# A hybrid short-convolution and state-space trunk on one core: the short mixer's output pairs for the first half of the sequence move ahead of the second half's input pairs, and the scan's first half is stored in seven forms

## The chip, the cores and the metric

One core of a Trainium2 chip. The metric is the device time of one execution in microseconds (us). TensorE is PE in the profile, its weight loads are PEld, VectorE is DVE, ScalarE is ACT, GpSimd is POOL. SP is the queue that issues nearly all transfers (DMAs) here.

## The reference, cut to what matters

Input x is 2048 positions by 1024 channels, f32. One layer and a closing norm:

```python
h = rmsnorm(x, norm_mix_w)
u_b, u_c, u_h, z, xbc, dt_raw = split(h @ w_in)          # w_in: 1024 x 5648
y_a = u_b * causal_conv3(u_c * u_h)                        # the short mixer, 1024 wide
xs, bm, cm = split(silu(causal_conv4(xbc) + conv_b))       # the scan's inputs
dt = softplus(dt_raw + dt_bias)
y = ssd_scan(xs, dt, -exp(a_log), bm, cm) + d_skip * xs    # 16 heads of 64, 2 groups, chunked
y_b = rmsnorm_per_group(y * silu(z), ssd_norm_w)           # 1024 wide, 2 groups of 512
x = x + concat(y_a, y_b) @ w_out                           # w_out: 2048 x 1024
x = x + relu(rmsnorm(x, norm_mlp_w) @ w_up) ** 2 @ w_down  # 4096 wide
out = rmsnorm(x, final_norm_w)
```

## The kernel before

**Layout.** Channels lie on the 128 partitions, positions along the free dimension. The sequence is cut into two halves of 1024 positions (h = 0, 1), each of two blocks of 512 (b = 0, 1 and b = 2, 3). All products are f32: each operand is split into a high and a low part (`whi`, `wlo` for weights, `uh`, `ul` for data), and three matmuls of 128x128 by 128x512 make one product (lines 293, 294, 295 in `chain`, lines 133 to 135 in `mm3`).

**Seven products for eight.** A "pair" is two output tiles of 128 channels over both blocks of a half: a 2x2 block product. `Seven.chain` does it with seven block products instead of eight, in the order b11, t1, t2, b21, t3, b22, t4. One product is 4 places of three matmuls, so a pair is 84 matmuls. For it the data must be there in seven forms, sums and differences of the four blocks (`uh0..uh3`, `ul0..ul3`: places 0 to 2 hold two forms each, place 3 the seventh), and the weights in four forms (`combine` makes the sums `s12`, `s34`). Results leave PSUM in `evict`, on DVE or ACT, product by product. The PSUM tiles px and py are each used by several products in turn, so a later product waits until the earlier one's result has been read.

**Stages.** (1) `first_half`: 20 pairs of w_in for h = 0. Pairs named ch and b make the short mixer and store its output in seven forms (`y7_d`); x pairs make the scan's inputs (`xs_d`); z pairs store silu(z) (`sz_d`). (2) `second_half`: the 22 pairs of `LATER` for h = 1, then 8 pairs o0 to o7 (`OUTS`) that multiply the short mixer's output by the first 1024 rows of w_out: o0 to o3 for h = 0, o4 to o7 for h = 1. Their results are added to x and stored in `x1_d`. (3) `Output`: 32 "units", one for each output tile of 128 channels and block of 512, which multiply the scan's output by the other rows of w_out: 8 places of three matmuls, 24 matmuls a unit, no sevens (PSUM tile pm). Units 0 to 15 are for b = 0, 1, units 16 to 31 for b = 2, 3. They add to `x1_d`; those of b = 0, 1 also add up the squares for the next norm. (4) The MLP, its two halves, and the closing norm.

**Turns.** Between groups of pairs the data operand changes. `renew` loads the seven forms of the next operand into the places as the last pair before frees them (L354: `ul<-y_d`), ACT makes the high part (L361) and DVE the low part (L362); places 2 and 3 are done in the next pair (`renew_rest`). There are two such turns in `second_half` (z4 to o0, o3 to o4), one change of the input half (`refresh`, at the end of the first half), and one into the units (`enter`).

**The scan** (`Scan`) runs beside the products on all engines. A chunk is 128 positions of one group of 8 heads; there are 32. `front` and `back` are generators that are advanced a step at a time (8 steps a chunk) from `after`, which `chain` calls behind each product: normally 8 steps a pair, fewer at a turn. On PE a chunk is the transposes ptx and ptb, the state product st, then yo, yd and, for its norm, pss. 27 chunks (`SPLIT`) run in `second_half` with single buffers (pool sp1). The last 5 run in the units 0 to 12 with a second pool (sp2, double buffers). Each chunk stores its gated and normalised output in `yn_d` (L1673).

**What sets the order.** The program is written in the order that the generators give, and a scheduling layer then places each instruction in its engine's queue. Each engine takes its own queue in order. SP's queue of DMAs is one such queue: a DMA that waits holds back those behind it.

Of the kernel before, what the change touches and what calls it, by code (L numbers as in the profile page):

```python
# [16 lines left out]
P = 128  # L17
T = 2048
D = 1024
TB = 512  # L20
# [19 lines left out]
def trunk(ctx: ExitStack, tc: tile.TileContext, x, x_tok, w_in, w_dt, w_out, w_up, w_down, cvec, hrow, out):  # L40
# [21 lines left out]
    xs_d, sz_d, yn_d = wide("xs", 12), wide("sz", 8), wide("yn", 8)  # L62
# [150 lines left out]
    class Seven:  # L213
# [158 lines left out]
        def prepare(self, h, src, base, accs=None, held=None):  # L372
# [32 lines left out]
            for k in range(4):  # L405
                ts = [held("nb") if held and i == 2 else self.raw("nb") for i in range(4)]
# [15 lines left out]
                if held:  # L422
                    self.held.append(ts[2])
                    nc.sync.dma_start(self.stored[h][k][:, 2:4], ts[1])
                    self.settle([self.places[k]], 0, [ts[0]])
# [29 lines left out]
    class Proj(Seven):  # L455
# [5 lines left out]
        LATER = "z6 x0 z0 ch0 ch4 b0 x8 ch1 ch5 b1 x2 ch2 ch6 b2 x10 z2 x4 x6 ch3 ch7 b3 z4".split()  # L461
        OUTS = "o0 o1 o2 o3 o4 o5 o6 o7".split()
# [30 lines left out]
        def tmp(self, name):  # L493
            return self.up.tile([P, TB], F32, tag="utmp", name=name, bufs=4 - 2 * self.h)
# [244 lines left out]
        def dt_weights(self):  # L739
# [3 lines left out]
            if self.h == 0:  # L743
                wdt = self.sumtile("wdt").bitcast(F32R)[:, 0 : KD * 32]
            else:
                wdt = self.up.tile([P, KD * 32], F32R, name="wdt")
# [106 lines left out]
        def pair(self, h, what, ws, ahead, after):  # L853
# [13 lines left out]
            elif kind == "o":  # L867
                return self.out_pair(n, ws, ahead, after)
# [70 lines left out]
        def residual(self, n, b):  # L939

            t = self.e("x0") if b == 0 else self.up.tile([P, TH], F32, tag="cc", name="x1", bufs=2)
            self.res[n, b] = t
            at = 2 * (n % 4)
            nc.sync.dma_start(t.rearrange("p (a t) -> p a t", a=2), x[n // 4 * NBB + b, :, at : at + 2])

        def out_pair(self, n, ws, ahead, after):
            b0, b1 = (self.res.pop((n, b)) for b in range(NBB))
# [3 lines left out]
            def evict(name, gi, pm):  # L951
# [10 lines left out]
                if fin:  # L962
                    nc.sync.dma_start(x1_d[n // 4 * NBB + b][:, 2 * (n % 4) + i], t)

            return self.chain([self.places], ws, ahead, evict, after)

        def renew(self, h, name):
# [3 lines left out]
            if name in ("t1", "b21", "b22", "t4"):  # L971
                i = ("t1", "b21", "b22", "t4").index(name)
                for k in range(4):
                    self.land(i, k, y7_d[h][k][:, 2 * i : 2 * i + (1 if i == 3 else 2)])
# [14 lines left out]
        def weights(self, h, what):  # L989

            if h == 0:
                if what != self.LATER[0]:
                    sums_d[what] = dram.tile([P, 2, 1024], F32, name=f"sums_{what}_d")
                raws = self.load_cols(w_in, self.cols(what))()
                yield
                yield from self.combine(*raws, sums_d.get(what))
# [12 lines left out]
            else:  # L1009
                f0, f1 = self.cols(what)  # L1010
            raw = lambda n, w=1024: wp.tile([P, 1024], F32, tag="wraw", name=n, bufs=3)[:, 0:w]
            r0 = load_w(w[f0])
            if what not in sums_d:
                r1 = load_w(w[f1])
                yield
                yield from self.combine(r0, r1)
                return
            s12, s34 = raw("s12"), raw("s34")
            nc.sync.dma_start(s12, sums_d[what][:, 0])
            nc.sync.dma_start(s34, sums_d[what][:, 1])  # L1020
# [3 lines left out]
            nc.sync.dma_start(a22.rearrange("p (k c) -> p k c", c=P), w[f1][:, KD // 2 :])  # L1024
# [3 lines left out]

        def first_half(self, ws):
            self.last_sums()  # L1030
            late = self.prepare(1, x, C_NMIX)
            for m, what in enumerate(self.PAIRS):
                last = m + 1 == len(self.PAIRS)
                if last:
                    for _ in late:
                        pass
                    ahead = None
                    self.new = [{} for _ in range(4)]
                else:
                    ahead = self.weights(0, self.PAIRS[m + 1])  # L1040
# [7 lines left out]
                ws = self.pair(0, what, ws, ahead, after) or ws  # L1048
# [3 lines left out]
        def second_half(self, ws, side):  # L1052

            self.dt_weights()
            dts = itertools.chain(*(self.dt_part(NBB + bb) for bb in range(NBB)))
            self.res = {}
            order = self.LATER + self.OUTS
            nl = len(self.LATER)
            turn = lambda m: m - nl in (-1, 3)
            for m, what in enumerate(order):  # L1060
                last = m + 1 == len(order)
                ahead = self.plain(w_out[1], (0, 1)) if last else self.weights(1, order[m + 1])

                def after(name):
                    if m or name == "t4":
                        next(dts, None)
                    at = m - nl
                    rest = at in (0, 4)
                    if name in LIGHT if turn(m) else name in LATE if rest else True:
                        for _ in range(1 + (name == "t3")):  # L1070
                            next(side, None)
                    if turn(m):
                        self.renew((at + 1) // 4, name)
                    elif rest:
                        self.renew_rest(name)
                    if m + 1 >= nl and not last and name in ("t1", "t3"):
                        self.residual(m + 1 - nl, ("t3", "t1").index(name))
# [4 lines left out]
                if turn(m):  # L1082
# [419 lines left out]
    SPLIT = 27  # L1502
    LIGHT, LATE = ("b11", "t3"), ("t3", "b22", "t4")

    class Scan:
# [45 lines left out]
        def load_rows(self, n):  # L1551
# [6 lines left out]
            if self.bufs == 1:  # L1558
                eb = self.tile([4, L], "eb", 1)
            else:  # L1560

                eb = uh.tile([P, 1, TB], F32R, tag="uh3", name="eb", bufs=4).bitcast(F32)
                eb = eb[:, 0].rearrange("p (j l) -> p j l", j=4)
            self.got[n]["eb"] = eb
# [54 lines left out]
        def back(self, n):  # L1619
# [22 lines left out]
            y = t["y"]  # L1642
# [360 lines left out]
```

## Time and profile before

| what | value |
|---|---|
| median of 3 runs | 2591.67 us (2590.14 to 2596.16) |
| the profiled execution's own time | 2592.11 us |
| its span | 2590.1 us |
| granted TensorE clock | 1.0 |
| PE busy, weight loads busy | 99%, 81% of the span |
| DVE, ACT busy | 75%, 54% |
| read and written in HBM | 364 MB, 187 MB |

PE's busy time is modelled: a matmul's record lasts longer than the time until the next one starts, so a stage is better judged by when its matmuls start and by what is left idle.

### The profile page before, as it was taken

To read this page: it belongs to the slowest core of one execution; us is meant where nothing else is said; L and a number is where in the kernel's file an instruction comes from. 1 tells how busy PE (TensorE), PEld (TensorE's weight loads), DVE (VectorE), ACT (ScalarE), POOL (GpSimd) and SP (SyncE) were. 2 spreads that over 40 slices of the span, in tenths; PEclk is the share of its full clock that TensorE was granted. 3 is DMA by queue.
4 is the path that set the end of the run, shared out by engine and by line. 5 is a ranking of instruction groups with operands and counts; after the bars stand their busy time and mean duration, and the time that the engine had idled before them with its cause. 6 is when DMAs were issued, how large, how long until landed. Compare 5 with 4: busy or idle time off the path is not lost.

```text
span 2590.1 us, 33610 instructions
## 1 busy us (share of the span) xinstructions
PE 2567.3 (99%) x11962; PEld 2109.2 (81%) x11962; DVE 1947.4 (75%) x2677; ACT 1405.0 (54%) x2171; POOL 66.5 (3%) x97
## 2 busy tenths in 40 slices
PE   9999999999999999999999999999999999999999
PEld 7888888778888887778888888888888888888887
DVE  7888776777888879778767765655558877877875
ACT  7554345776577765547336555655556444444443
POOL 0011000000000000000000000000000000000001
PEclk9999999999999999999999999999999999999999
DMA  5557535555656669989765774744448766676872
GB/s 215 204 202 278 204 139 185 186 179 189 194 172 198 193 220 313 328 272 285 239 211 183 261 255 147 259 143 159 154 147 284 260 203 207 225 236 218 281 252 78
DMA packets 295623, 553.87 MB, mean 214 GB/s; under 512 B 26272, under 2 KB 142496, under 8 KB 295456
## 3 DMA queue, kind: packets, MB, share of 16 engines
q1 hardware_dynamic: 295024, 551.34, 62.7%
q8 instruction: 94, 1.54, 0.2%
q14 instruction: 73, 0.60, 0.1%
q10 hardware_dynamic: 432, 0.39, 0.0%
HBM read 364.46 MB, written 187.17 MB: 213 GB/s over the span
## 4 chain that ended last, share of the span: by engine, by line
PE 85%; DMA 6%; DVE 5%; ACT 2%; issue 1%; SPq 0%; DVEq 0%; ACTq 0%
PE px L293 14%; PE px L295 14%; PE px L294 14%; PE py L293 7%; PE py L295 7%; PE py L294 7%; PE pw L293 3%; PE pw L295 3%; PE pw L294 3%; PE pm L133 3%; PE pm L134 3%; PE pm L135 3%; PE pm L510 1%; PE yd L1635 1%; PE yo L1632 1%
## 5 line engine op out<-in xcount | busy, mean ns | idle before, releaser
L293 PE MATMUL px<-uh,whi 128*128 128x512 f32 x1800 | 705.0, 392 | 3.4 <-DVE x L961 1.5
L294 PE MATMUL px<-ul,whi 128*128 128x512 f32 x1800 | 701.7, 390 | 0.2 <-DVE ul L362 0.2
L295 PE MATMUL px<-uh,wlo 128*128 128x512 f32 x1800 | 700.6, 390 | 0.6 <-DVE wlo L110 0.6
L293 PEld LDWEIGHTS px<-uh,whi 128*128 128x128 f32 x1800 | 337.9, 188 | 78.3 <-DVE acc L1314 2.8
L295 PEld LDWEIGHTS px<-uh,wlo 128*128 128x128 f32 x1800 | 337.9, 188 | 71.9 <-DVE wlo L110 1.7
L294 PEld LDWEIGHTS px<-ul,whi 128*128 128x128 f32 x1800 | 338.0, 188 | 70.0 <-DVE ul L362 1.8
L109 ACT CAST whi<-s 128x1024 fp32r<-128x1024 f32 (+1 forms) x222 | 232.2, 1046 | 276.2 <-PE py L294 147.5
L110 DVE TENSOR_TENSOR wlo<-wraw,whi 128x1024 fp32r<-128x1024 f32 (+1 forms) x220 | 219.5, 998 | 184.5 <-ACT whi L109 182.7
L293 PE MATMUL py<-uh,whi 128*128 128x512 f32 x900 | 354.7, 394 | 1.4 <-ACT s L1111 0.8
L295 PE MATMUL py<-uh,wlo 128*128 128x512 f32 x900 | 351.6, 391 | 0.0
L294 PE MATMUL py<-ul,whi 128*128 128x512 f32 x900 | 351.0, 390 | 0.0
L110 DVE TENSOR_TENSOR wlo<-s,whi 128x1024 fp32r<-128x1024 f32 (+1 forms) x222 | 269.8, 1215 | 70.7 <-ACT whi L109 69.4
L109 ACT CAST whi<-wraw 128x1024 fp32r<-128x1024 f32 (+1 forms) x220 | 191.9, 872 | 226.1 <-PE px L294 163.4
L293 PEld LDWEIGHTS py<-uh,whi 128*128 128x128 f32 x900 | 169.0, 188 | 39.5 <-issue 3.3
L295 PEld LDWEIGHTS py<-uh,wlo 128*128 128x128 f32 x900 | 169.0, 188 | 35.6 <-issue 0.3
L294 PEld LDWEIGHTS py<-ul,whi 128*128 128x128 f32 x900 | 169.0, 188 | 34.1 <-issue 0.2
L349 DVE TENSOR_TENSOR ul<-rh,uh 128x1024 fp32r<-128x1024 f32 (+1 forms) x128 | 138.7, 1086 | 49.6 <-ACT uh L348 49.2
L293 PE MATMUL pw<-uh,whi 128*128 128x512 f32 x450 | 175.4, 390 | 0.0
L295 PE MATMUL pw<-uh,wlo 128*128 128x512 f32 x450 | 175.3, 390 | 0.0
L294 PE MATMUL pw<-ul,whi 128*128 128x512 f32 x450 | 175.3, 389 | 0.0
L348 ACT CAST uh<-rh 128x1024 fp32r<-128x1024 f32 (+1 forms) x128 | 119.9, 944 | 92.7 <-PE py L295 57.3
L301 ACT COPY pw<-px 128x512 f32<-128x512 f32 x118 | 67.6, 573 | 114.3 <-PE px L295 113.1
(261 smaller groups left out, 3672.4 us busy)
## 6 DMA issues: line engine op xcount, KB each, us to landing
hid_d<-e SPq DMA_DIRECT2D x96, 512.0 KB, 3.6
rh<-hid_d SPq DMA_DIRECT2D x96, 512.0 KB, 4.6
wraw<-w_in SPq DMA_DIRECT2D x67, 512.0 KB, 4.5
wraw<-w_up SPq DMA_DIRECT2D x62, 512.0 KB, 4.4
wraw<-w_down SPq DMA_DIRECT2D x88, 256.0 KB, 4.2
dec<-rd_d SPq DMA_DIRECT2D x32, 512.0 KB, 5.1
wraw<-w_out SPq DMA_DIRECT2D x28, 512.0 KB, 5.8
x<-x SPq DMA_DIRECT2D x24, 512.0 KB, 6.8
```

Of the source, the lines that this page charges most:

```text
L109: nc.scalar.copy(hi, raw)
L110: eng.tensor_tensor(out=lo, in0=raw, in1=hi.bitcast(F32), op=ALU.subtract)
L133: nc.tensor.matmul(out, whi, hi, start=(k == 0), stop=False)
L134: nc.tensor.matmul(out, whi, lo, start=False, stop=False)
L135: nc.tensor.matmul(out, wlo, hi, start=False, stop=(k == nk - 1))
L293: nc.tensor.matmul(p, hi, h[0], start=bool(first and k == 0), stop=False, **kw)
L294: nc.tensor.matmul(p, hi, h[1], start=False, stop=False, **kw)
L295: nc.tensor.matmul(p, lo, h[0], start=False, stop=(k == len(g) - 1), **kw)
L301: self.copied = nc.scalar.copy(pm[gi]["w"], pm[gi]["x"]).ins
L348: nc.scalar.copy(p[i][0], t)
L349: nc.vector.tensor_tensor(out=p[i][1], in0=t, in1=p[i][0].bitcast(F32), op=ALU.subtract)
L510: last[engine] = make(*args, **kw).ins
```

## The change

1. Order of `second_half`: o0 to o3 (`FORMER`) come first, then `LATER` in another order, then p0 to p3 and o4 to o7. The first half now ends with a turn to the short mixer's output (`y7_d[0]`), and `second_half` has three turns: o3 to x0 (the second input half, `hm_d[1]`, whose seven forms the first half stored as before), b3 to p0 (the scan's first half, `yb7`), p3 to o4 (`y7_d[1]`).
2. p0 to p3 are new pairs: the scan's output for h = 0 times its rows of w_out, by seven products. They replace units 0 to 15. They take `x1_d` as what is added to, and also do the squares for the next norm (`square`).
3. The scan writes its first half (b = 0, 1) in the seven forms (`yb_d`) instead of `yn_d`: chunks of b = 0 store two forms, chunks of b = 1 load those again (into the tile xd), make four differences on DVE and store them.
4. `gate_weights`, in the first half, multiplies the scan's rows of w_out by ssd_norm_w, makes the weight sums and stores them (`wy_d`). Before, the gain was applied to the data (`cut`).
5. One scan pool: all 32 chunks run in `second_half` with single buffers. What is left of the scan before the last pair, o7, is written at once ahead of it. z pairs advance the scan by 10 steps instead of 8.
6. The units left are 16, for b = 2, 3, two output tiles at a time in the order (2, d), (2, d+1), (3, d), (3, d+1). The MLP's preparation runs beside them as before, and holds back place 0 instead of place 2 until unit 13.

The instructions counted in the two programs: 384 matmuls of the units go (128 in each of three lines) and 336 of pairs come; DMAs go from 1505 to 1590, DVE instructions from 2679 to 2763, ACT instructions from 2167 to 2180.

```diff
     def __init__(self): ...
-        LATER = "z6 x0 z0 ch0 ch4 b0 x8 ch1 ch5 b1 x2 ch2 ch6 b2 x10 z2 x4 x6 ch3 ch7 b3 z4".split()
-        OUTS = "o0 o1 o2 o3 o4 o5 o6 o7".split()
+        LATER = "x0 z0 x8 z2 x2 ch0 ch4 x10 b0 z4 ch1 ch5 x4 b1 z6 x6 ch2 ch6 b2 ch3 ch7 b3".split()
+        FORMER = "o0 o1 o2 o3".split()
+        OUTS = "p0 p1 p2 p3 o4 o5 o6 o7".split()
...
         def first_half(self, ws):
-            late = self.prepare(1, x, C_NMIX)
+            late = itertools.chain(self.prepare(1, x, C_NMIX), self.gate_weights())
...
-                        self.refresh(name)
+                        self.renew(y7_d[0], name)
...
         def second_half(self, ws, side):
-            order = self.LATER + self.OUTS
-            turn = lambda m: m - nl in (-1, 3)
+            order = self.FORMER + self.LATER + self.OUTS
+            nf, nl = len(self.FORMER), len(self.FORMER) + len(self.LATER)
+            turns = {nf - 1: hm_d[1], nl - 1: yb7, nl + 3: y7_d[1]}
...
-                        for _ in range(1 + (name == "t3")):
+                        for _ in range(1 + (name == "t3") + (what[0] == "z" and name in ("t1", "b21"))):
                             next(side, None)
...
+                    if not last and order[m + 1][0] in "op":
+                        at = {"t4": (1, 0)} if what[0] == "b" else {"t1": (1,), "t3": (0,)}
+                        for b in at.get(name, ()):
+                            self.residual(order[m + 1], b)
...
+                if last:
+                    for _ in side:
+                        pass
...
         # in Scan.back, at the end
-            nc.sync.dma_start(yn_d[h][:, 4 * g : 4 * g + 4, ts], y)
+            if h:
+                nc.sync.dma_start(yn_d[:, 4 * g : 4 * g + 4, ts], y)
+                yield
+                return
...
+            if b == 0:
+                for i in range(2):
+                    put(3 * i, 1, y[:, 2 * i : 2 * i + 2])
+            else:
+                yp, s = t["xd"], self.tmp().rearrange("p (j l) -> p j l", j=4)
+                sub(s[:, lo], y[:, lo], yp[:, lo])
+                sub(y[:, lo], y[:, hi], y[:, lo])
+                sub(s[:, hi], y[:, hi], s[:, lo])
+                sub(t4, yp[:, hi], s[:, hi])
+                put(1, 2, s)
+                put(4, 2, y)
+                put(6, 1, t4)
...
         # in Output
-        UNITS = [(b, d) for d in range(KD) for b in ((0, 1) if d < 7 else (1, 0))] + [(b, d) for d in range(KD) for b in (2, 3)]
+        UNITS = [(b, d + i) for d in range(0, KD, 2) for b in (2, 3) for i in range(2)]
...
-            side = scan.run(0, SPLIT)
+            side = scan.run(0, len(CHUNKS))
             ws = proj.second_half(ws, side)
...
-            scan.open(c2, "sp2", 2)
-            side = scan.run(SPLIT, len(CHUNKS))
-            for n in range(13):
-                proj_out.unit(n, hook)
```

**On DVE, at the turn into the first output pairs behind the input pairs.** Before, this is z4 to o0; `x<-py` and `x<-px` (L961) empty o0's PSUM tiles, `ul` of L362 are the low parts of the new operand, the 128x512 ones those of place 3.

```order
L362 TENSOR_TENSOR ul_8599<-ul_8599,uh_8598 128x1024
L961 TENSOR_TENSOR x_8548<-py,x_8548 128x512
L1652 TENSOR_TENSOR state_3787<-state_3787,dd 128x512
L1654 TENSOR_TENSOR stmp<-yo,eb 128x512
L961 TENSOR_TENSOR x_8548<-px,x_8548 128x512
L362 TENSOR_TENSOR ul_8668<-ul_8668,uh_8667 128x1024
L1653 TENSOR_TENSOR state_3787<-state_3787,st 128x512
L362 TENSOR_TENSOR ul_8671<-ul_8671,uh_8670 128x1024
L961 TENSOR_TENSOR x_8642<-pw,x_8642 128x512
L362 TENSOR_TENSOR ul_8674<-ul_8674,uh_8673 128x1024
```

After, it is b3 to p0; L985 empties p0's PSUM tiles and L366 makes the low parts.

```order
L366 TENSOR_TENSOR ul_9729<-ul_9729,uh_9728 128x1024
L366 TENSOR_TENSOR ul_9732<-ul_9732,uh_9731 128x1024
L366 TENSOR_TENSOR ul_9735<-ul_9735,uh_9734 128x1024
L366 TENSOR_TENSOR ul_9762<-ul_9762,uh_9761 128x512
L366 TENSOR_TENSOR ul_9765<-ul_9765,uh_9764 128x512
L366 TENSOR_TENSOR ul_9768<-ul_9768,uh_9767 128x512
L1725 TENSOR_TENSOR stmp<-stmp 128x256
L366 TENSOR_TENSOR ul_9771<-ul_9771,uh_9770 128x512
L1727 TENSOR_TENSOR ssq<-stmp 128x128
L985 TENSOR_TENSOR x_9777<-py,x_9777 128x512
L985 TENSOR_TENSOR x_9777<-px,x_9777 128x512
```

The first two evictions stood ahead of the low parts of places 2 and 3; now they stand behind all of them.

**On PE, where the scan ends.** Before, a late chunk's products (st, yo, yd) stand among the matmuls of a unit (pm), and the norm's pss of the chunk ahead of it follows.

```order
L135 MATMUL pm<-uh_10186,wlo 128x512
L133 MATMUL st<-xde,btok 128x512
L134 MATMUL st<-xde,btok 128x512
L135 MATMUL st<-xde,btok 128x512
L1632 MATMUL yo<-bc,state_3788 128x128 x4
L1635 MATMUL yd<-dec,stmp 64x128 x8
L1667 MATMUL pss<-ssq,ones_r 128x128
L133 MATMUL pm<-uh_10177,whi 128x512
```

After, the last two chunks stand in the last pair, o7 (its first product writes this px): chunk 30's products and already the transposes of chunk 31.

```order
L1730 MATMUL pss<-ssq,ones_r 128x128
L297 MATMUL px<-uh_10447,whi 128x512
L298 MATMUL px<-ul_10448,whi 128x512
L299 MATMUL px<-uh_10447,wlo 128x512
L297 MATMUL px<-uh_10450,whi 128x512
L137 MATMUL st<-xde,btok 128x512
L1651 MATMUL ptx<-ident,xd 128x128 x4
L298 MATMUL px<-ul_10451,whi 128x512
L1691 MATMUL yo<-bc,state_3889 128x128 x4
L138 MATMUL st<-xde,btok 128x512
L139 MATMUL st<-xde,btok 128x512
L1694 MATMUL yd<-dec,stmp 64x128 x8
```

Chunk 31's own yd stands 42 large matmuls further on, still in o7; before, a late chunk's yd stood 48 behind the one ahead of it.

**On SP, behind the last chunk.** Before, the scan's last store (L1673) is followed by the units' own transfers, and only units from the 17th on read what it stores. After, L1737 is that store and L1810 loads it for the units of b = 3.

```order
L1673 DMA yn_d_102<-y 128x4x128
L1828 DMA x_d_77<-xt 128x512
L1755 DMA ry<-yn_d_102 128x2x512 x2
L1801 DMA xt<-x_d_77 128x512
L1828 DMA x_d_78<-xt 128x512
```

```order
L1737 DMA yn_d<-y 128x4x128
L105 DMA wraw<-w_out 128x1024
L1840 DMA xt<-x_d_79 128x512
L1810 DMA ul_11441<-yn_d 128x2x512
L1810 DMA ul_11444<-yn_d 128x2x512
L1810 DMA ul_11447<-yn_d 128x2x512
L1810 DMA ul_11450<-yn_d 128x2x512
```

The loads stand two rows behind the store, and the third unit, the first of b = 3, reads them.

More of the change, by code (lines that the diff above doesn't have):

```diff
@@ L866, in pair @@
                 nc.gpsimd.tensor_copy(b[:, 0:2], self.halo_s[:, n, :])
[L867 to L868 removed]
+            elif kind in "op":
+                return self.out_pair(what, ws, ahead, after)
             else:
@@ L1045, in after @@
                     if last:
-                        self.refresh(name)
-                ws = self.pair(0, what, ws, ahead, after) or ws
+                        self.renew(y7_d[0], name)
+                ws = self.pair(0, what, ws, ahead, after)
             self.places = self.new
```

287 lines of the change are left out of this document (135 added, 152 removed).

## The prediction

> **What bounds the kernel now.** First the page: span, busy shares, chain.
>
> ```profile
> span 2590.1 us, 33610 instructions
> PE 2567.3 (99%) x11962; PEld 2109.2 (81%) x11962; DVE 1947.4 (75%) x2677; ACT 1405.0 (54%) x2171; POOL 66.5 (3%) x97
> PE 85%; DMA 6%; DVE 5%; ACT 2%; issue 1%; SPq 0%; DVEq 0%; ACTq 0%
> ```
>
> PE is the bound at full clock; DVE is the next engine. Since PE's busy time is modelled, I looked up when pairs start. Columns: start, duration, engine, operation.
>
> ```profile
> 308.16 0.39 PE L293 MATMUL pw<-uh,whi 128*128 128x512 f32 x1
> 327.20 0.39 PE L293 MATMUL pw<-uh,whi 128*128 128x512 f32 x1
> ...
> 702.56 0.39 PE L293 MATMUL pw<-uh,whi 128*128 128x512 f32 x1
> 725.41 0.39 PE L293 MATMUL pw<-uh,whi 128*128 128x512 f32 x1
> ```
>
> The first two are one pair apart without scan work: 327.20 - 308.16 = 19.04 us for 84 matmuls, 0.2267 us each. The last two are one pair with one chunk of the scan apart, 22.85 us, so a chunk takes 3.81 us of PE. A matmul removed is worth 0.2267 us, not its recorded 0.39.
>
> Then the stages: first half, its last turn, two early stretches of the second half, its steady part, the output pairs with their turns, the units with the scan's last 5 chunks, the units without. Columns: window, its length, busy time of PE, PEld, DVE, ACT, POOL, PE clock, DMA share, GB/s.
>
> ```profile
> 79.00:441.00 362.00, 361.63 (x1598) 298.97 (x1597) 285.34 (x359) 167.14 (x210) 32.56 (x38) 1.00 0.55 196
> 441.00:490.00 49.00, 47.88 (x229) 36.88 (x228) 34.72 (x51) 38.67 (x70) 2.09 (x2) 1.00 0.77 253
> 490.00:545.00 55.00, 53.05 (x276) 41.50 (x275) 43.60 (x90) 42.52 (x72) 1.01 (x4) 1.00 0.49 155
> 545.00:952.00 407.00, 405.23 (x2124) 334.05 (x2123) 333.28 (x470) 272.41 (x516) 17.25 (x34) 1.00 0.59 185
> 952.00:1144.00 192.00, 186.77 (x917) 150.70 (x916) 155.05 (x216) 109.95 (x187) 0.00 (x0) 1.00 0.90 313
> 1144.00:1242.00 98.00, 95.97 (x519) 79.62 (x518) 80.71 (x129) 60.60 (x130) 0.00 (x0) 1.00 0.87 274
> 1242.00:1336.00 94.00, 94.00 (x417) 77.82 (x416) 67.42 (x89) 25.78 (x33) 0.00 (x0) 1.00 0.72 242
> ```
>
> Idle time of PE is length less busy: 0.37, 1.12, 1.95, 1.77, 5.23, 2.03 and 0.00 us, 12.1 us from 441 on. That is all the waiting that the changed part can lose; it may also grow. Inside the output pairs:
>
> ```profile
> 960.00:1003.00 43.00, 40.83 (x194) 32.11 (x193) 41.27 (x55) 33.51 (x49) 0.00 (x0) 1.00 0.91 324
> 1060.00:1084.00 24.00, 23.27 (x112) 17.84 (x111) 20.90 (x27) 13.95 (x16) 0.00 (x0) 1.00 0.81 321
> 1084.00:1144.00 60.00, 57.67 (x290) 46.81 (x290) 41.22 (x63) 26.81 (x56) 0.00 (x0) 1.00 0.87 285
> ```
>
> The turn z4 to o0 costs 2.17 us, with DVE busy 41.27 of 43 us; o3 to o4 costs 0.73; entering the units 2.33.
>
> **The change, part by part.** *Matmuls.* 384 go, 336 come: 48 x 0.2267 = -10.9 us. The scan's matmuls are unchanged. The squares' matmuls change line, not number.
>
> *DVE in the first half and the scan.* The rows that price DVE, and those of ACT that a chunk waits for (line, engine, tiles, count, then total us and mean ns):
>
> ```profile
> L232 DVE TENSOR_TENSOR nb<-nb 128x512 f32<-128x512 f32 x16 | 10.5, 685 | 0.0
> L1662 DVE TENSOR_TENSOR stmp<-stmp 128x256 f32<-128x256 f32 x32 | 13.4, 419 | 5.3 <-ACT stmp L1661 5.1
> L362 DVE TENSOR_TENSOR ul<-ul,uh 128x1024 fp32r<-128x1024 f32 x24 | 28.7, 1217 | 0.9 <-ACT uh L361 0.9
> L362 DVE TENSOR_TENSOR ul<-ul,uh 128x512 fp32r<-128x512 f32 x8 | 5.1, 682 | 0.0
> L961 DVE TENSOR_TENSOR x<-px,x 128x512 f32<-128x512 f32 x24 | 16.5, 685 | 4.7 <-PE px L295 4.6
> L1616 DVE TENSOR_TENSOR dec<-dec,smask 128x1024 f32<-128x1024 f32 x32 | 39.0, 1220 | 9.9 <-ACT dec L123 9.8
> L1672 DVE TENSOR_TENSOR y<-y,ssq 128x512 f32<-128x512 f32 x32 | 21.9, 684 | 10.0 <-ACT ssq L1670 9.9
> L1610 ACT ACTIVATE dec<-dec,dd 128x128 f32<-128x128 f32 x256 | 85.4, 392 | 25.8 <-DMA dec<-rd_d 25.0 <-DMA dd<-dt_d 0.7
> L123 ACT ACTIVATE dec<-dec 128x1024 f32<-128x1024 f32 x32 | 33.9, 1059 | 0.6
> L123 ACT ACTIVATE ssq<-pss,hb 128x128 f32<-128x128 f32 x32 | 11.6, 363 | 6.9 <-PE pss L1667 6.8
> L1670 ACT ACTIVATE ssq<-ssq 128x128 f32<-128x128 f32 x32 | 9.8, 307 | 0.6
> L1781 ACT ACTIVATE uh<-ul,cv 128x512 fp32r<-128x512 f32 x16 | 10.4, 712 | 7.4 <-DMA ul<-yn_d 7.4
> ```
>
> `gate_weights` adds 32 DVE instructions of 128x512, the size of the `nb` row: 32 x 0.685 = 22 us. DVE there goes from 285 to 307 of 362 us, 85%; PE still waited only 1.77 us in the steady stretch where DVE was 82% busy (333.28 of 407). I take nothing, and keep 1 us. The differences of `yb_d`: 8 chunks x 4 instructions of 128x256 at 0.419 us = 13.4 us in the steady part, which has some 70 us of DVE left over: nothing. If that cover went, up to 13 us would show. The load of `xd` back from `yb_d` is needed only at the chunk's end, behind the scan's other work: nothing.
>
> *z pairs at 10 steps* move scan work earlier and change no sum.
>
> *Turn z6 to o0* (the end of the first half). The first evictions (two of 0.685) stand behind the low parts again, and the scan has hardly begun, so I take about what the turn of the input half cost (1.12) to what z4 to o0 cost (2.17): 2 us at most, 1.2 taken.
>
> *New turn o3 to x0.* Before there was none inside these pairs. Nearest row: the input half's turn, 1.12. Bounds 0.7 and 2.2; 1.1 taken.
>
> *Turn b3 to p0.* On DVE, behind b3's last product, now come its eviction, a weight's low part and t24 (3 x 0.685), six splits of 1.217, four of 0.682, two small ones (0.42, 0.2) and only then p0's first eviction (0.685): 2.1 + 7.3 + 2.7 + 0.6 + 0.7 = 13.4 us. PE has 48 matmuls (10.9) and the scan's transposes, 12.0 us in all, before it needs that PSUM tile. On SP the residual stands behind the last loads of the operand, which stand behind the store of t24, which waits on DVE. Transfers in the crowded stretch, from the chain (start, duration, transfer):
>
> ```profile
> 1047.27 9.02 DMA x<-x
> ...
> 1065.41 7.65 DMA ul<-y_d
> ...
> 1103.70 4.95 DMA yn_d<-y
> ...
> 1134.28 5.81 DMA ul<-yn_d
> ```
>
> 2.3 us of DVE until t24, then 9.02 for a residual, then the eviction: 12.0, about the same cover, if it lands like that row. So 1.5 us by DVE alone, more with queueing: bounds 1 and 6, 4 taken, since the similar old turn had a shorter DVE row and paid 2.17.
>
> *Turn p3 to o4.* As o3 to o4 (0.73) plus up to 4 squares of 0.685 on DVE: 0.7 to 3.4, 1.2 taken. Two steady waits of about 2 us (490:545, 545:952) stay: 2 + 2.
>
> *The scan's end.* The pairs offer 241 steps, the scan needs 4 + 32 x 8 = 260; 19 steps, 2.4 chunks, are written at once ahead of o7. From yd of chunk 30 to yd of chunk 31: the decay's load, 4.95 (the nearest transfer of that size), 8 activations (0.392 alone, some 0.31 apart when back to back: 2.5 to 3.1), exponential 1.06, mask 1.22 = 10.0 us; PE has 42 matmuls, 9.5. Behind the last pss: 0.36 + 0.31 + 0.68, store 4.95, load 5.81, scaling 0.71 = 12.8 us against 42 matmuls, 9.5. So 0.5 + 3.3, and about 1 for queueing: 5 us, where the entry into the units and their part with the scan cost 2.33 + 2.03 = 4.4. Bounds: 2 (the load lands early) and 10 (each of the three transfers takes some 2 to 3 us longer, as 9.02 against 5.81).
>
> Waits after: 1.2 + 4 + 1.1 + 4 + 1.2 + 5 = 16.5 us, against 12.1: +4.4. Sum: -10.9 + 4.4 = -6.5. Against the profiled execution's own 2592.11 (2 us outside its span) that gives 2585.6; the median of the runs is 0.4 lower, so 2585.2 to 2585.6, **2585.5 us**. About 0.2%, 5.2 us, can be told from no change: faster is below 2586.5, slower above 2596.9.
>
> Transfers as a bound: the output stretch already moves 313 GB/s at 0.90. By the program's tile sizes about 62.5 MB now move there instead of about 60 (313 x 192), over some 200 us: no new bound, but no room.
>
> PE's weight loads weigh on whether removing matmuls saves time at all:
>
> ```profile
> L293 PEld LDWEIGHTS px<-uh,whi 128*128 128x128 f32 x1800 | 337.9, 188 | 78.3 <-DVE acc L1314 2.8
> ```
>
> A load of 188 ns in each 226.7 ns is 83%, so the page's 81% is what an unbroken stream shows here. The Trainium skill, "Perfetto Trace Analysis", section "Identifying the Most-Contended Engine", holds the share of LDWEIGHTS, not of matmuls, to be the measure of closeness to the limit, by which 81% would leave room. The trace doesn't bear that out. By the Trainium skill, "TensorE: Matmul & The Clock Gate", section "Back-to-back issue gap", sustained matmuls of N = 512 come about 131 ns apart: 48 of them would be an estimated 6.3 us rather than 10.9. No stretch of this trace has them that close; the starts above are 226.7 apart.
>
> **The rivals.**
> *R1, turns and end eat the gain.* Four turns at 2.2 to 6 and the end at its worst: 2.2 + 2.2 + 6 + 2.2 + 8 + the steady 4 = 24.6, less 12.1, = +12.5 at the extreme; a middle course, waits of 21 to 22, gives 2592.1 - 10.9 + 9.5 = 2590.7. For it: DVE at 41.27 of 43 us. Against: each turn so far cost at most 2.3.
> *R2, slower: the drained scan.* From yd of chunk 29 to the first unit of b = 3 runs one chain: 10.0 + 10.0, then some 5 for that chunk's y, gate and squares, 12.8: 38 us bare. PE has 172 matmuls and the chunks' own, 43 us. With the extra steps at once in front of o7, transfers and in-order DVE and SP queues may stretch it. From 59 us on PE waits 16 us, and the time passes 2597; with 21, about 2602. For it: nothing lies between but o7 and two units, and in the steady stretch DVE is busy 82%, 18.7 us, of a pair with one chunk, while here 2.4 chunks go beside less than two pairs. Against: the chain's own rows, 38 us, leave 5 us of cover, and PE is never idle in 1242:1336, where the units load the same operand.
> *R3, no growth of waits.* 2592.1 - 10.9 = 2581.2, 2580.8 on the median, for which every new turn would have to be hidden, as the first half's pairs hide DVE at 79%.
> *R4, matmuls save nothing,* as PE isn't the limit: only the waits' 4.4 is left, less a little, 2595. Against it 94.00 of 94.00 us busy.
>
> **How the numbers follow.** Forecast (2583 to 2586.5) 0.50, R3 0.06: faster 0.56. R1 0.24 and R4 0.04: same 0.28. R2 0.16: slower 0.16. The range runs from R3's 2580.8 with a wait less, 2580, to R4's 2595; R2 is outside. Its own range for the likeliest case is 2582 to 2589 by the bounds of the two largest waits (-3, +3 about).
>
> **What would show it.** Right: pairs still 19.04 and 22.85 us apart; some 48 fewer large matmuls; 3 to 6 us of PE idle at b3 to p0, on p0's px or py waiting for DVE; 0.7 to 2 at the other turns; 3 to 6 between o7 and the third unit, `ul<-yn_d` named. Wrong: idle of 8 us or more at p0 (R1); 16 or more at o7 or the third unit (R2); pairs longer than 22.85 in the first or second half (DVE has become the limit); starts closer than 0.2267 (R4).

## The result: 1.1% slower, and where the waits came from

The changed kernel takes 2621.98 us (median of 4 runs, 2620.74 to 2622.92), the kernel before 2593.53 (median of 4): ratio 1.011, 95% interval 1.0093 to 1.0128, some 28 us slower. The forecast was 2585.5. Every ratio below is to executions of the kernel before made beside that run (medians 2594.35 for the first four, 2598.3 and 2597.05 for the others). One execution of the first experiment was in a slow state (11222.63 us) and is left out of its ratio. First the page of the changed kernel.

```profile
span 2620.1 us, 33808 instructions
PE 2568.7 (98%) x11914; PEld 2106.3 (80%) x11914; DVE 1996.0 (76%) x2761; ACT 1425.2 (54%) x2184; POOL 65.8 (3%) x97
```

48 matmuls fewer are there (x11914 against x11962), and yet the span is 30 us longer. So time was added between or within the matmuls that are left. The stages of the changed kernel (length, then busy PE, PEld, DVE, ACT, POOL, granted clock, DMA share, GB/s): first half, its turn to o0, o1 and o2, the end of o3 to x8, the middle input pairs, the last five, b3 to p0, p1 to o4, the end with the scan's last chunks.

```profile
79.00:441.00 362.00, 361.11 (x1591) 297.67 (x1590) 302.15 (x392) 163.00 (x205) 35.01 (x38) 1.00 0.64 227
441.00:490.00 49.00, 42.80 (x186) 34.14 (x184) 36.45 (x43) 30.79 (x46) 0.00 (x0) 0.97 0.90 312
490.00:545.00 55.00, 54.91 (x289) 45.11 (x288) 45.96 (x69) 30.21 (x63) 0.38 (x2) 1.00 0.89 300
545.00:640.00 95.00, 88.62 (x438) 68.74 (x437) 78.85 (x134) 77.18 (x120) 4.44 (x6) 0.98 0.59 199
640.00:960.00 320.00, 307.86 (x1594) 251.33 (x1593) 257.20 (x386) 220.72 (x412) 9.56 (x26) 0.99 0.65 200
960.00:1080.00 120.00, 119.86 (x622) 99.00 (x621) 91.19 (x128) 73.43 (x143) 2.84 (x6) 1.00 0.61 197
1080.00:1140.00 60.00, 53.35 (x263) 43.10 (x262) 53.88 (x76) 35.91 (x63) 0.00 (x0) 0.94 0.91 306
1140.00:1215.00 75.00, 72.31 (x355) 58.59 (x354) 64.34 (x91) 45.77 (x76) 0.00 (x0) 1.00 0.84 289
1215.00:1310.00 95.00, 88.47 (x445) 71.12 (x444) 71.66 (x105) 46.26 (x90) 0.00 (x0) 0.98 0.83 270
```

Idle time of PE, length less busy, is 0.89, 6.20, 0.09, 6.38, 12.14, 0.14, 6.65, 2.69 and 6.53 us, 41.7 in all. The same middle stretch of the kernel before, 640 to 960 us, which also holds input pairs only, serves as a gauge from here on:

```profile
640.00:960.00 320.00, 318.23 (x1657) 262.28 (x1657) 263.51 (x371) 218.22 (x413) 13.20 (x26) 1.00 0.61 192
```

1.77 us idle before, 12.14 now. The clock column (1.00 is the full granted clock) shows a second loss: it is below 1.00 in five rows. Taken from the starts of all matmuls between 100 and 1345 us (each start against the usual step of its kind), waits of over 0.45 us sum to 45.7 us in the changed kernel and 13.5 before, and smaller delays, nearly all of them matmuls at half clock, to 11.4 against 2.1. That is 41.5 us more, less 10.9 us of matmuls: 30.6, the 30.0 by which the span grew.

**Turn b3 to p0.** PE there (start, duration, line, operation, and what it waited for):

```profile
1100.02 0.40 PE L299 MATMUL pw<-uh,wlo 128*128 128x512 f32 x1
1106.71 0.77 PE L1730 MATMUL pss<-ssq,ones_r 128*128 128x128 f32 x2 [6.30 <-DVE ssq L1727]
...
1108.30 0.63 PE L297 MATMUL px<-uh,whi 128*128 128x512 f32 x1
1108.73 0.63 PE L298 MATMUL px<-ul,whi 128*128 128x512 f32 x1
...
1110.93 0.40 PE L298 MATMUL px<-ul,whi 128*128 128x512 f32 x1
1111.17 0.39 PE L299 MATMUL px<-uh,wlo 128*128 128x512 f32 x1
```

(pss is the PSUM tile of the scan's norm, ssq the sum of squares that it reads.) DVE at that time:

```profile
1094.74 0.68 DVE L862 TENSOR_TENSOR eb<-px,cc 128x512 f32<-128x512 f32 x1
...
1096.54 8.70 DVE L366 TENSOR_TENSOR ul<-ul,uh 128x1024 fp32r<-128x1024 f32 x9
1105.16 0.42 DVE L1725 TENSOR_TENSOR stmp<-stmp 128x256 f32<-128x256 f32 x1
1105.67 0.69 DVE L366 TENSOR_TENSOR ul<-ul,uh 128x512 fp32r<-128x512 f32 x1
1106.28 0.28 DVE L1727 TENSOR_TENSOR ssq<-stmp 128x128 f32<-128x128 f32 x1
1106.48 0.68 DVE L985 TENSOR_TENSOR x<-py,x 128x512 f32<-128x512 f32 x1
```

Nine splits run in one block, the scan's ssq and p0's first eviction stand behind them, and PE waits 6.3 us for ssq. Ssq is not alone in being late: the residual that this eviction adds was issued at 1099.79 and landed at 1106.23, just ahead of 1106.48. So a shorter row on DVE alone would not have let the product that next needs py start much sooner. And behind the wait the matmuls start 0.427 us apart, not 0.227, until 1110.4. The granted clock around it:

```profile
1099.00:1103.00 4.00, 1.41 (x7) 0.80 (x5) 4.00 (x4) 1.80 (x4) 0.00 (x0) 1.00 0.99 318
1103.00:1107.00 4.00, 0.29 (x1) 0.32 (x2) 3.91 (x8) 1.21 (x2) 0.00 (x0) 0.58 0.97 367
1107.00:1111.00 4.00, 4.00 (x12) 3.13 (x12) 4.00 (x9) 2.87 (x5) 0.00 (x0) 0.56 1.02 413
1111.00:1115.00 4.00, 4.00 (x19) 3.31 (x18) 3.40 (x5) 1.01 (x2) 0.00 (x0) 1.00 0.67 214
```

**Other places.** Waits of PE in the turn to o0, between o3 and x8, and at the end (what waits, for what; sum, times, longest). Under the first, the eviction on DVE that it waits for:

```profile
PE py L297 <- DVE x L985: 5.6, 2, 4.6
```

```profile
468.06 0.69 DVE L985 TENSOR_TENSOR x<-py,x 128x512 f32<-128x512 f32 x1 [0.29 <-DMA x<-x]
```

```profile
PE px L297 <- ACT pw L305: 2.8, 1, 2.8
```

```profile
PE pm L137 <- ACT uh L1820: 3.0, 2, 2.1
PE st L137 <- ACT xde L1639: 1.9, 1, 1.9
```

The last two lines are the end of the scan: the units of b = 3 wait for their operand, and a chunk's state product for its own. The stretch has 6.53 us of idle time, some 8 with the half clock in it, not the 16 of the slower rival.

### The profile page after: what moved, and what is told of

Read it like the earlier page. It is cut to its first block, busy times and chain, and to the rows that moved or that the text cites. A ratio compares the mean times of both kernels' runs of the same rounds, so it can differ in the third digit from the quotient of the medians.

```text
span 2620.1 us, 33808 instructions
## 1 busy us (share of the span) xinstructions
PE 2568.7 (98%) x11914; PEld 2106.3 (80%) x11914; DVE 1996.0 (76%) x2761; ACT 1425.2 (54%) x2184; POOL 65.8 (3%) x97
## 4 chain that ended last, share of the span: by engine, by line
PE 60%; DMA 6%; ACT 4%; DVE 3%; issue 1%; SPq 0%; DVEq 0%; ACTq 0%
PE px L297 10%; PE px L298 10%; PE px L299 10%; PE py L297 5%; PE py L298 5%; PE py L299 5%; PE pw L297 3%; PE pw L299 3%; PE pw L298 3%; DMA dec<-rd_d 2%; PE pm L137 2%; PE pm L138 1%; PE pm L139 1%; ACT dec L1669 1%; DMA yn_d<-y 1%
## 5 line engine op out<-in xcount | busy, mean ns | idle before, releaser
L297 PE MATMUL px<-uh,whi 128*128 128x512 f32 x1864 | 733.7, 394 | 9.1 <-ACT pw L305 7.2
L298 PE MATMUL px<-ul,whi 128*128 128x512 f32 x1864 | 728.6, 391 | 2.4 <-DVE ul L366 2.3
L299 PE MATMUL px<-uh,wlo 128*128 128x512 f32 x1864 | 727.8, 391 | 0.0
L297 PEld LDWEIGHTS px<-uh,whi 128*128 128x128 f32 x1864 | 351.0, 188 | 91.7 <-ACT pw L305 11.2
L298 PEld LDWEIGHTS px<-ul,whi 128*128 128x128 f32 x1864 | 351.1, 188 | 75.5 <-DVE ul L366 4.5
L299 PEld LDWEIGHTS px<-uh,wlo 128*128 128x128 f32 x1864 | 350.9, 188 | 73.6 <-issue 0.3
L113 ACT CAST whi<-s 128x1024 fp32r<-128x1024 f32 x232 | 242.4, 1045 | 222.2 <-PE py L298 88.3
L114 DVE TENSOR_TENSOR wlo<-s,whi 128x1024 fp32r<-128x1024 f32 x232 | 282.0, 1216 | 75.0 <-ACT whi L113 73.9
L114 DVE TENSOR_TENSOR wlo<-wraw,whi 128x512 fp32r<-128x512 f32 (+3 forms) x213 | 211.0, 991 | 158.2 <-ACT whi L113 157.5
L113 ACT CAST whi<-wraw 128x512 fp32r<-128x512 f32 (+3 forms) x213 | 184.5, 866 | 241.4 <-PE px L298 167.0
```

The source lines that it names most:

```text
L113: nc.scalar.copy(hi, raw)
L114: eng.tensor_tensor(out=lo, in0=raw, in1=hi.bitcast(F32), op=ALU.subtract)
L297: nc.tensor.matmul(p, hi, h[0], start=bool(first and k == 0), stop=False, **kw)
L298: nc.tensor.matmul(p, hi, h[1], start=False, stop=False, **kw)
L299: nc.tensor.matmul(p, lo, h[0], start=False, stop=(k == len(g) - 1), **kw)
```

## The experiments

"Place" below is the step of a scan chunk (0 to 7) with which an input pair begins. Two readings of the middle stretch are set against each other: by the load theory, the extra work of the change makes its waits; by the phase theory, the place does. The place follows from counting steps: before, the first pair writes 4 steps of preparation and 4 of chunk 0, and with 8 steps a pair every later pair begins with step 4. In the changed kernel the turns and the 10 steps of z pairs make it 7 in z0, then 1, 3, 5 and 7. What PE does in 640 to 960 us, and the ratio to the kernel before with its interval:

| run | place in the middle stretch | PE idle, 640 to 960 us | ratio |
|---|---|---|---|
| before | 4 | 1.77 | 1 |
| changed | 1, 3, 5, 7 | 12.14 | 1.011 (1.0093 to 1.0128) |
| e1_phase | 0 | 11.55 | 1.0097 (1.0073 to 1.0121) |
| e2_noforms | as changed | 11.52 | 1.0109 (1.009 to 1.0129) |
| e3_behind | 0 | 10.63 | 1.0097 (1.0082 to 1.0112) |
| e4_before_shift | 6 | 14.18 | 1.012 (1.0103 to 1.0137) |
| e12_before_shift1 | 5 | 10.72 | 1.0091 (1.0072 to 1.0109) |
| e8_before_late | 4, a chunk later | 2.88 | 1.0001 (0.9992 to 1.0011) |
| e5_phase4 | 4 | 5.57 | 1.0066 (1.004 to 1.0091) |
| e6_behind4 | 4 | 4.27 | 1.0016 (1.0007 to 1.0026) |
| e7_twochunks | 4 | 5.93 | 1.0006 (0.9993 to 1.0018) |
| e11_pool | 4 | 13.64 | 1.0052 (1.0035 to 1.0069) |
| e9_after_relu | as changed | 8.76 | 1.0066 (1.0045 to 1.0088) |
| e10_shift_relu | 6 | 2.78 | 0.9998 (0.9986 to 1.0009) |

**1. The steps in z pairs.**

```diff
-  for _ in range(1 + (name == "t3") + (what[0] == "z" and name in ("t1", "b21"))):
+  for _ in range(1 + (name == "t3") + (m == nf and name == "t4")):                 # x0 5 steps, z pairs 8
```

> Changed kernel, but z pairs advance the scan by 8 steps as all others do, and x0 by one step more, so that each input pair behind z0 begins at the same place of a chunk as in the kernel before. Phase theory (where a chunk's steps fall beside a pair's own ACT and DVE work makes the waits of the middle stretch, 16 us between 640 and 1060 us against 2 to 4 before): these waits fall to 4 to 6 us; 26 steps instead of 19 are then written at once ahead of o7, which costs some 4 us there; time about 2615. Load theory (the extra work of the store in seven forms makes them): the middle stretch stays at 14 to 18 us, time 2622 to 2627.

11.55 us idle, 1.0097: nothing gained. The expectation rested on a miscount: with these steps the pairs begin at place 0, not 4. So it decides nothing between the two theories; the run with the right count is the fifth.

**2. Without the differences of the seven forms.** The reload of block 0's result and the four `sub` of block 1 are left out; the stores put `y` in their place.

> Changed kernel that leaves out, for the chunks of block 1, the load of block 0's result and the four differences; the three stores stay, with the plain result in them. Load theory: the waits of the middle stretch fall from 16 to under 6 us, time about 2611. Phase theory: they fall by at most 3 us (8 chunks x 4 x 0.42 us of DVE less, on an engine that isn't full there), time 2618 to 2622.

1.0109 with 11.52 us idle: the load theory falls as far as it rests on the four differences and the reload. The stores in more pieces stayed, so they are not tested by this run.

**3. The order of before, with seven products.**

```diff
-  self.renew(y7_d[0], name)
+  self.renew(hm_d[1], name)                           # at the end of the first half
...
-  order = self.FORMER + self.LATER + self.OUTS
+  order = self.LATER + self.FORMER + self.OUTS        # LATER as before, 8 steps a pair
...
```

> Changed kernel with the former order put back: the first half ends with the turn to the second input half, then the input pairs in the order of before with 8 steps a pair, then o0 to o3, p0 to p3, o4 to o7; seven products for p0 to p3, the seven forms and the one scan pool stay. If order and phase make the waits: middle stretch 4, first turn and dt part 4 instead of 17.7, the turns z4 to o0 3, o3 to p0 7, p3 to o4 3, end 10 (23 steps at once): 31 us of waits instead of 55, time about 2598. If the seven forms or the new pairs make them wherever they stand: the middle stretch keeps 14 or more and the time is 2610 or more.

1.0097 (2621.7 us), far from the 2598 of the first branch: neither branch of the expectation saw that the first pair, now one behind a turn, writes 4 steps instead of 8, and that all input pairs so begin at place 0.

**4. Two steps more in the kernel before.** The one that decided.

```diff
-  for _ in range(1 + (name == "t3")):
+  for _ in range(1 + (name == "t3") + (m == 0 and name in ("t1", "b21"))):
```

> Kernel before, with two scan steps more in its first input pair z6 and nothing else, so that all input pairs behind it begin two steps further on in a chunk. Phase theory: the waits of the steady stretch grow from some 4 us by 3 to 10, time 2596 to 2603. Load theory: nothing is added, so no change, 2591 to 2595.

1.012: with no matmul, transfer or DVE instruction added (x11962 and x2677 as before), the kernel before becomes slower by as much as the whole change made it. The phase theory was right in kind and three times too low in size: some 31 us against 10 at most. Its gauge row:

```profile
640.00:960.00 320.00, 305.82 (x1561) 248.65 (x1560) 245.19 (x342) 221.50 (x398) 16.32 (x26) 0.98 0.56 173
```

ACT there, ahead of PE's longest wait in this stretch:

```profile
643.43 1.06 ACT L126 ACTIVATE cacc<-cacc 128x1024 f32<-128x1024 f32 x1 [1.04 <-DVE cacc L838]
644.51 1.28 ACT L120 ACT_TABLE_LOAD   x1
645.80 0.37 ACT L123 ACTIVATE ssq<-pss,hb 128x128 f32<-128x128 f32 x1
646.19 1.28 ACT L126 ACT_TABLE_LOAD   x1
647.48 1.06 ACT L126 ACTIVATE cacc<-cacc 128x1024 f32<-128x1024 f32 x1
648.56 1.28 ACT L1670 ACT_TABLE_LOAD   x1
649.85 0.31 ACT L1670 ACTIVATE ssq<-ssq 128x128 f32<-128x128 f32 x1
650.18 1.28 ACT L120 ACT_TABLE_LOAD   x1
651.48 1.06 ACT L123 ACTIVATE dec<-dec 128x1024 f32<-128x1024 f32 x1
652.44 0.57 ACT L882 COPY s<-py 128x512 f32<-128x512 f32 x1
```

and PE:

```profile
653.06 0.50 PE L293 MATMUL py<-uh,whi 128*128 128x512 f32 x1 [2.53 <-ACT s L882]
```

Line 126 is the silu of the input pair, 123 and 1670 are the scan's logarithm and exponentials. They need different function tables, and each change is a load of 1.28 us. At place 6 they alternate: four loads, 5.1 us, in the 8 us ahead of the copy that empties py (L882), and PE stands still until that copy is done. (The fourth, L120, is a load that the kernel itself asks for; it follows an exponential, with no silu between.) In the whole stretch there are 28 loads, against 16 in the kernel before. The Trainium skill, "ScalarE: Activation LUTs", section "Table sets: the hidden batching unit", says to group activations by table set and not by function. The tenth run below bears it out here. The kernel before adds a limit: its 16 loads leave PE with 1.77 us idle, so a load costs PE only where something that PE needs stands behind it.

**5. Place 4 in the changed kernel.**

```diff
-  for _ in range(1 + (name == "t3") + (what[0] == "z" and name in ("t1", "b21"))):
+  for _ in range(1 + (name == "t3") + (m == nf and name == "t4") + (m in (1, 2) and name in ("t1", "b21"))):
```

x0 takes 5 steps, o1 and o2 take 10, z pairs 8.

> Changed kernel; z pairs advance the scan by 8 steps, o1 and o2 by 10, x0 by 5 instead of 4. Counted step by step, each input pair behind x0 then begins with step 4 of a chunk, as every pair does in the kernel before (in the run without the two steps in z pairs it was step 0, in the changed kernel 7, 1, 3, 5 and 7 in turn, in the kernel before with two steps more it was 6). Phase theory: waits between 640 and 1060 us fall from some 14 to 4 to 6 us; 22 steps at once at the end instead of 19; time 2608 to 2614. If the place in the chunk isn't what counts: the middle stretch keeps 12 or more, time 2620 or more.

5.57 us idle in the stretch and 1.0066, as expected: of the 28 us some 11 go when the place is put back.

**6. Order, first turn and place of before.** As the third, but the first half ends with `refresh` as before, and the first pair has its 8 steps.

> Changed kernel with the order of before put back and the turn to the second input half done as before (loaded ahead into tiles of its own, the scan advanced by 8 steps in the first pair), so that all 22 input pairs begin with step 4 of a chunk. Seven products for p0 to p3, seven forms, one pool, the end at once (23 steps) stay. Phase theory: first turn 1.5, middle stretch 4, z4 to o0 3, o3 to p0 5 to 7, p3 to o4 3, end 13 to 15: 30 to 34 us of waits against 15.5, less 10.9 of matmuls: 2596 to 2602. If order and phase aren't it: 2615 or more.

1.0016. Against the third run this takes away 21 us (1.0097 to 1.0016 of 2598), through the place (10.63 to 4.27 us idle) and the first turn (4.66 to 1.40 us idle in 441 to 490 us, both times into the second input half).

```profile
640.00:960.00 320.00, 315.73 (x1640) 258.53 (x1639) 273.17 (x403) 218.25 (x410) 13.70 (x26) 1.00 0.67 204
```

At the new turn, now o3 to p0, no wait is longer than 0.9 us, where behind b3 it was 6.3. That fits DVE's backlog in b3, which makes the short mixer's own differences; the turn was not changed by itself.

**7. Two chunks each in o5 and o6.**

```diff
-  for _ in range(1 + (name == "t3")):
+  for _ in range((1 + (name == "t3")) * (1 + (what in ("o5", "o6")))):
```

> As the run before it, with 16 scan steps instead of 8 in o5 and in o6, so that 7 steps instead of 23 are left for the end ahead of o7. If what is written at once makes the end's waits (13 to 15 us in the earlier run with this order of pairs): they fall to 5 to 8, two pairs whose DVE work (some 28 us) is about their PE time (26.7) add 2 to 4; time 5 to 8 us less than the run before it, 2589 to 2596. If the end's waits come from the last chunk's chain alone (norm, store, load, scaling), they stay, and the time is the same within 3 us.

1.0006 (0.9993 to 1.0018), level with the kernel before. It is some 2.6 us less than the sixth, half of what was expected, and the two intervals overlap. The end's waits are gone (none over 0.6 us from 1232 us on); one of 2.2 us in o6, one of the two fuller pairs, has come.

**8. The kernel before, scan one whole chunk later.** No steps in the first pair, `SPLIT = 26`.

> Kernel before, with the scan started one input pair later (a whole chunk, 8 steps; the units take 6 chunks instead of 5). From the third input pair on each pair begins with step 4 of a chunk as before, though the scan is 8 steps behind. Phase theory: steady stretch unchanged at some 4 us; 2591 to 2599. If any move of the scan against the pairs costs, as the two steps more did (+33 us): 2610 or more.

1.0001. Eight steps cost nothing where two cost 31 us: it is the place in the chunk, not the move.

```profile
640.00:960.00 320.00, 317.12 (x1643) 260.54 (x1642) 262.21 (x369) 217.27 (x405) 12.70 (x26) 1.00 0.62 193
```

**9 and 10. No function tables to change.** Relu for silu in the second half, in the changed kernel and in the fourth run's.

```diff
   def silu(out, in_):
+      if proj.h:                                      # the second half
+          nc.scalar.activation(out, in_, AF.Relu)
+          return
       table[0] = nc.scalar.activation(out, in_, AF.Silu).ins
```

> Changed kernel that leaves out the silu of the second half (relu in its place, same instruction count and sizes), so that ACT needs no change of its function table between the scan's exponentials and the pairs' work. Table theory (ACT's in-order queue loses 1.28 us at each table load, and PE's evictions and chunk steps behind it wait): PE's idle time in 640 to 960 us falls from 12.1 to 5 or less, time 2603 to 2611. Place theory without tables (steps of a chunk queue behind the pair's own instructions on ACT and DVE whatever the table): idle 9 to 12 us, time 2614 to 2621.

> Kernel before with two scan steps more in its first input pair, and the silu of the second half left out in the same way. Table theory: of the 33 us that the two steps cost, 20 or more go: idle in 640 to 960 us from 14.2 to 5 or less, time 2598 to 2608. Without tables as the cause: idle 10 or more, time 2618 to 2628.

The tenth: 0.9998, the whole 1.2% is gone.

```profile
640.00:960.00 320.00, 317.22 (x1645) 260.90 (x1644) 255.74 (x364) 193.77 (x388) 21.58 (x26) 1.00 0.62 186
```

At place 6 the wait needs the loads: without one in the stretch, 2.78 us idle are left of 14.18. (The kernel before without silu was not run; with 1.77 us idle it had little to gain there.) The ninth fell between the two theories: 1.0066, some 11 us gained, the wait of 2.8 us for ACT in x8 gone, yet 8.76 us idle remain in the stretch. PE's waits there, and what DVE did ahead of the longest one, which ended at 754.79:

```profile
PE pss L1733 <- DVE ssq L1730: 5.8, 5, 2.0
PE px L300 <- ACT pw L308: 2.9, 3, 1.5
```

```profile
749.44 5.00 DVE L846 SCALAR_TENSOR_TENSOR cacc<-buf,cv,cacc 128x1024 f32<-128x1024 f32 x4
754.36 0.28 DVE L1730 TENSOR_TENSOR ssq<-stmp 128x128 f32<-128x128 f32 x1
```

Four of the pair's own convolution steps, 5.0 us, stand on DVE ahead of the scan's ssq. At places 1, 3 and 5 PE so waits with no load in the stretch; the other waits were not traced one by one.

**11. The four differences on POOL.**

> The order of before with seven products for the first half and two chunks each in o5 and o6 (the run at 1.0006 of the kernel before), with the four differences of the seven forms on POOL instead of DVE. If DVE's extra load in the middle stretch is what is left of the waits there (5.9 us idle in 640 to 960 against 1.8 before): idle 3 to 4 us, ratio to the kernel before 0.998 to 1.000. If POOL is slow or is in DVE's way: no change or slower, 1.000 to 1.003.

1.0052, worse, beyond the worse branch. Each takes 1.0 to 1.1 us there instead of 0.42:

```profile
L1749 POOL TENSOR_TENSOR stmp<-y,xd 128x256 f32<-128x256 f32 x8 | 9.0, 1126 | 86.5 <-DVE y L1734 55.2 <-PE yo L1690 18.1 <-ACT xs L1672 8.9
```

PE then waits more for ssq and the decay, 13.64 us idle. Why the waits spread beyond the chunks concerned was not traced. Since POOL was slower, the run doesn't settle whether DVE's extra work makes the 5.93 us of the seventh.

**12. One step more in the kernel before.** `(m == 0 and name == "t1")`.

> Kernel before with one scan step more in its first input pair instead of two, so that each later pair begins with step 5 of a chunk. If the cost grows with the distance from step 4: half of the 33 us, time 2605 to 2615. If only certain steps meet the table loads and evictions badly: as little as no change (2592 to 2600) or as much as two steps (2620 or more).

1.0091, 24 us for one step, where two cost 31: more than the half of the first branch and less than the second's worst. Only 12 table loads lie in the stretch there, fewer than the 16 of the kernel before. Its longest wait is for another thing in the same queue:

```profile
PE px L293 <- ACT pw L301: 3.1, 2, 2.7
```

```profile
721.46 0.99 ACT L1610 ACTIVATE dec<-dec,dd 128x128 f32<-128x128 f32 x3 [4.58 <-DMA dec<-rd_d]
```

The copy of px, at 728.70, stands on ACT behind the scan's eight relus (0.39 us each) and the pair's own casts and convolution steps, and the first relu waited 4.58 us for the load of the decay. So the number of table loads isn't the measure. What counts is what stands ahead of an eviction in ACT's and DVE's in-order queues when PE comes for it, and that is set by the place, together with what the pair itself does: the changed kernel's last five input pairs (ch and b) begin with place 7, only 2 table loads lie between 960 and 1080 us, and PE idles 0.14 us there.

**The load of the decay.** These relus make ACT wait for that load all over the middle stretch. Its waits in 640 to 960 us (sum, times, longest) in the kernel before, the changed one and the twelfth run:

```profile
ACT dec L1610 <- DMA dec<-rd_d: 6.9, 8, 2.0
ACT dec L1669 <- DMA dec<-rd_d: 22.3, 10, 3.8
ACT dec L1610 <- DMA dec<-rd_d: 42.9, 12, 7.1
```

At place 4 (fifth to eighth runs) they are 8.7 to 13.1 us, at place 6 26.1 (fourth run). In the tenth run they are still 24.1, with PE idle for 2.78 us only, so by themselves they needn't stop PE. No run takes them away, so their share in the changed kernel's 12.14 us is open.

## Why the prediction was wrong

- **Matmuls, right.** 48 fewer; pairs without waits are still 22.85 us long (ch1: 816.0 to 838.8).
- **"z pairs at 10 steps move scan work earlier and change no sum", and the two steady waits that "stay: 2 + 2": wrong, the largest step.** From 490 to 1080 us PE is idle for 18.75 us (0.09, 6.38, 12.14, 0.14), where 4 and the 1.1 of the turn to x0 were taken. That is 13.6 of the 24.3 us by which all idle time behind 441 us, 40.8, exceeds the 16.5 forecast. The fourth, fifth and eighth runs show why: each turn and each z pair changes the place at which later pairs begin. The argument was by load (DVE has 70 us left over); the second run agrees that the four differences cost nothing there. But an engine with time left over can still be late: its queue is in order, and what PE needs may stand behind other work.
- **Turn z6 to o0, 1.2 taken, 2 the bound: 6.2 idle.** x is added behind the last low parts, which wait for ACT and it for the loads; the residual x itself landed 0.29 us later still. The bound came from z4 to o0 (2.17) and from a turn that loads ahead (1.12). With the loads ahead again, into the second input half (sixth run), 1.40 us are idle in that window.
- **Turn b3 to p0, 4 taken, 6 the bound: 6.65 idle.** The chain of DVE rows was counted from the moment that b3's last product ended, with DVE free. DVE was then busy without a gap since 1079 and took up that product's result, ready at some 1087.5, only at 1094.74; over half of the cover of 12.0 us was by then used. The path through the residual, given about the same length, came out as late (1106.23). Its 2.3 us until t24 should have been 2.1 by its own row; that changes nothing.
- **o3 to x0, 1.1:** the turn itself is near that (a wait of 1.3 us at 562 us); x8, two pairs after x0, where ACT makes the second half's dt among table loads, is not.
- **Turn p3 to o4, 1.2 taken, 3.4 the bound:** 2.69 idle from p1 to o4, within its bounds.
- **The end, 5 taken, 10 the bound:** 6.5 idle, some 8 with the half clock. The mechanism (store, load, scaling) was right.
- **Half clock, no term at all.** Five stretches of about 8 matmuls with 0.2 us more each, some 8 us. So a wait of 2.6 us costs some 4 us.
- **The rivals.** R1 came nearest in kind, the turns and end ate the gain, but it held the middle for untouched. R2's mechanism was there and not its size. R4 is out: the matmuls that are left still start 0.2267 us apart where nothing waits, and the account above closes with the 10.9 us taken off (30.6 against 30.0). R1's extreme takes 8 us for the end, though 10 was its bound. No rival came near 2622: the highest time named was R2's 2602.

What stays open: how the 13 us between the fifth run and the sixth (1.0066 to 1.0016) divide among the turns, since only the order as a whole was put back. The share of table loads, of the decay's load and of DVE's queue in the middle waits of the changed kernel is open too: without silu some 11 us go (ninth run), and the rest was not taken apart.

## What to carry to other kernels

Work that is woven step by step into a periodic stream has a phase. Before costing a change by engine load alone, count at which step of its cycle it will meet each period of the stream, and keep that place; add or drop whole cycles, not steps. If it must move, look at what stands ahead of each eviction on the in-order engines, table loads first.

Seven products for the first half can be had at no measurable loss (the seventh run), but no gain was left either: the 10.9 us went into waits elsewhere, 5.93 instead of 1.77 us in the middle stretch among them. Which part of the change makes them was not shown.

## What the runs showed of the hardware

- The granted clock fell to 0.50 at waits of PE of 2.5 us and more in the changed kernel (at 464, 612, 666 and 1100 us; the rows at 1103 and 1107 above) and at one of 2.1 with one of 0.9 ahead of it (1299 us), and some 3 us of matmuls ran at it. It did not at waits of 1.9 and 2.0 us (1257 and 890 us), nor at one of 2.5 in the fourth run (650 us). But it did at one of 2.2 in that run (747 us), of 1.8 in the seventh (509 us) and of 1.6 in the twelfth (638 us). So the length of the wait alone doesn't decide it here. The Trainium skill, "TensorE: Matmul & The Clock Gate", section "Part 1: The HAM clock gate (the "warmup" mystery)", gives half clock after at least one idle window of about 3.4 us and about as long to come back. The length of the slow stretch agrees with this trace. A shorter wait suffices here, as the 1.6 us show.
- A table load took 1.28 us in every run, and a 128x256 difference 0.42 us on DVE and 1.0 to 1.1 on POOL.
